# One stage of a hybrid decoder layer: a costed order of issue with GpSimd's instructions holding VectorE too, and normed tokens in natural order

## The chip, the cores and the metric

The kernel runs on one core of one Trainium2 chip. The metric is the device time of one execution in microseconds (us), as the median of several runs. A core has TensorE (PE, with its weight loads as PEld), VectorE (DVE), ScalarE (ACT), GpSimd (POOL), SyncE (SP) and 16 DMA engines. Each engine runs its own instructions in the order in which the program issued them; it waits at an instruction whose operands another engine has not finished.

## What is computed

A decoder layer on 2048 tokens of width 1024: two token mixers share an input projection (they end before the stage spoken of here), then an output projection with a residual, a norm, a router and a mixture of 64 small gated MLPs, two for each token:

```
rwkv7_mixer:  y = groupnorm(y) * ln_w + ln_b;  return (y + bonus) * g        # 512 wide, 8 heads
y_mix = concatenate([y_rw, y_fox]);  x = x + y_mix @ w_out
h = rms_norm(x, norm_ffn_w)
g_sel = argmax(h @ rg_w + rg_b)                 # one of 8 groups
top_p, top_i = top_k(softmax((h @ re_w + re_b)[g_sel]), 2)
x = x + sum over the 2 experts e of gate_e * (silu(h @ w_gate[e]) * (h @ w_up[e])) @ w_down[e]
```

## The kernel before

Products are made in float16 from pairs: a value is split into a high half (a cast) and a low half (value minus high), and three products of halves are summed. The kernel ends with two stages that matter here.

The first is `mix`, from about 1390 to 1705 us. It works through 16 tiles of 128 tokens. For each tile: GpSimd makes the bonus term (L1547, L1548); `head_norm` normalises the heads on DVE (L1493 to L1508); GpSimd applies the norm's weight and adds the bonus (L1568, L1569); DVE multiplies by the gate (L1573); ACT and DVE split the result into halves (L1576, L1578), PE transposes it (L1584) and multiplies it by the output weights (L1625 to L1627); DVE adds the residual (L1639); ACT squares and sums (L1650), small DVE steps make the inverse root, and L1661 writes the normed tile `h32` (128 tokens by 1024, float32). ACT casts `h32` into the high half (L1669) and DVE subtracts to get the low half (L1671). Both read `h32` through a rearranged view, so that the halves lie k-major: element n = 8q + k goes to place (k, q). The halves are stored to memory (`h2d`, L1683), and PE transposes them in 8 blocks of 128 contiguous columns each, 16 transposes a tile (L1686); the tile is the stationary operand (a weight load), the identity the moving one. The router's products (L1695, L1697) give logits, `place` picks groups and experts on DVE (L1712 to L1765), and GpSimd scatters each token's entry into a table (L1769).

The order of issue in `mix` is not that of the code. `Lanes` holds generators; each yields what it needs next: an engine with a cost in us (`"D", 0.6` is 0.6 us of VectorE, P GpSimd, A ScalarE, T TensorE), a buffer, or a mark of other work. The recorder keeps a clock for each engine and always issues the step that can start first by these costs; steps that tie go by the order of the lanes. The costs are written by hand and decide nothing but the order; on the chip, each engine takes the order as it stands.

The second is `experts`, from about 1730 us to the end, with a recorder of its own. For each of 64 experts: an indirect DMA gathers up to 112 tokens' halves from `h2d` into `XG`; PE transposes them, 8 blocks for each half, 16 an expert (L2110); DVE copies them out (L2113); ACT and DVE split the weights, of which each expert has 12 pieces of 128 by 1024 (L1975 high, L1979 low); PE multiplies (L2152 to L2154, then L2145 to L2147). The weights stream from memory all the while. Four of the L1979 steps of the first experts are issued inside `mix`, at its end (`split_first`), and the lines L1973 and L1975 likewise.

Of the kernel before, what the change touches and what calls it, by code (L numbers as in the profile page):

```python
# [12 lines left out]
AF = mybir.ActivationFunctionType  # L13
# [6 lines left out]
D = 1024  # L20
# [9 lines left out]
SL = 112  # L30
# [13 lines left out]
class Lanes:  # L44

    def __init__(self, slots, order=()):
        self.lanes = {k: [] for k in order}  # L50
        self.free, self.marks, self.end = {}, {}, 0.0
        self.slots = {k: [0.0] * n for k, n in slots.items()}
# [22 lines left out]
    def run(self):  # L75
        while any(self.lanes.values()):
            best = None
            for q in self.lanes.values():
                if q:
                    what, t = q[0][1], q[0][2]  # L80
                    if isinstance(what, tuple):
                        t = max(t, self.free.get(what[0], 0.0))
                    elif what in self.slots:
                        if not self.slots[what]:
                            continue
                        t = max(t, self.slots[what][0])
                    elif what in self.marks:
                        t = max(t, self.marks[what])
                    else:
                        continue  # L90
                    if best is None or t < best[0]:
                        best = t, q, what
            t, q, what = best
            if isinstance(what, tuple):
                self.free[what[0]] = t + what[1]
                t += what[1] + (0.13 if what[0] != "T" else 0)
            elif what in self.slots:
                self.slots[what].pop(0)
            q[0][2] = self.end = t
            self.step(q)  # L100


class Kern:
# [1410 lines left out]
    def mix(self):  # L1514
# [13 lines left out]
        with ExitStack() as es:  # L1528
# [10 lines left out]
            def bonus(i):  # L1539
# [4 lines left out]
                yield f"vt{i}"  # L1544
                yield "P", 2.2
                s["bo"] = bo = wf.tile([128, 512], F32, name="gbo")
                nc.gpsimd.tensor_tensor(h8(bo), h8(V), bc(bon), op=OP.mult)  # L1547
                nc.gpsimd.tensor_tensor(bo, bo, row["rw_ln_b"], op=OP.add)  # L1548
                lanes.mark(f"bo{i}")
# [7 lines left out]
            def gate(i):  # L1557
# [8 lines left out]
                yield f"bo{i}"  # L1566
                yield "P", 2.5
                nc.gpsimd.tensor_tensor(y, y, row["rw_ln_w"], op=OP.mult)  # L1568
                nc.gpsimd.tensor_tensor(y, y, s["bo"], op=OP.add)  # L1569
                lanes.mark(f"y{i}")  # L1570
                yield "D", 0.6
# [3 lines left out]
                yield "A", 0.52  # L1575
                nc.scalar.activation(yh[:, 0], y, AF.Copy)  # L1576
                yield "D", 0.6
                TT(yh[:, 1], y, yh[:, 0], op=OP.subtract)  # L1578
# [52 lines left out]
            def residual(i, hf):  # L1631
                s = St[i]
                if hf == 0:
                    if i >= 2:
                        yield f"normed{i - 2}"
                    s["xm"] = xms[:, i % 2]
                yield "D", 0.6
                c = slice(hf * 512, hf * 512 + 512)
# [6 lines left out]
            def route(i):  # L1645
# [10 lines left out]
                yield "D", 0.08  # L1656
                for _ in self.rsqrt1_steps(wk, r, s["ss"]):
                    yield "D", 0.08
# [6 lines left out]
                yield "A", 0.95  # L1665

                h16 = h16s[:, i % 2]
                hv = h32.rearrange("p (q k) -> p k q", k=KB)
                nc.scalar.activation(h16[:, 0], hv, AF.Copy)  # L1669
                yield "D", 1.2  # L1670
                nc.vector.tensor_tensor(h16[:, 1], hv, h16[:, 0], op=OP.subtract)  # L1671
                lanes.mark(f"low{i}")
                lanes.start("logits", logits(i, h16))

            def logits(i, h16):
# [3 lines left out]
                for m in range(2):  # L1679
                    yield "sm"  # L1680
                    yield "T", 0.45
                    if m == 0:
                        nc.sync.dma_start(self.h2d[i * 128:(i + 1) * 128], h16.rearrange("p s k q -> p (s k q)"))  # L1683
# [3 lines left out]
                    yield "A", 0.9  # L1687
                    nc.scalar.activation(hT[:, m], pt, AF.Copy)
# [19 lines left out]
            def place(i, lg):  # L1708

                yield "D", 0.08  # L1710
                m8 = wk.tile([128, 8], F32, name="m8")
                nc.vector.max(m8, lg[:, 0:8])  # L1712
                yield "D", 0.08
                i8 = wk.tile([128, 8], U32, name="i8")
                nc.vector.max_index(i8, m8, lg[:, 0:8])
                yield "D", 0.08
# [4 lines left out]
                yield "D", 0.13  # L1721
                pen = wk.tile([128, 8], F32, name="pen")
                TS(pen, iof[:, 0:8], gf, -1e30, op0=OP.not_equal, op1=OP.mult)
                yield "D", 0.13
# [3 lines left out]
                yield "D", 0.13  # L1728
# [3 lines left out]
                yield "D", 0.13  # L1732
                e8 = wk.tile([128, 8], U32, name="e8")
# [26 lines left out]
                lanes.give("sm")  # L1760
                yield "D", 0.08
                STT(pos, pos, float(E), ef, op0=OP.mult, op1=OP.add)
                yield "D", 0.08
                ri = wk.tile([128, 2], I32, name="ri", bufs=2)
# [9 lines left out]
            def weigh(i, lg, ng, zz):  # L1774
# [4 lines left out]
                nc.scalar.activation(zz, zz, AF.Exp)  # L1779
                yield "D", 0.08  # L1780
                dn = wk.tile([128, 1], F32, name="dn")
                TS(dn, zz[:, 1:2], 1.0, sg, op0=OP.add, op1=OP.mult)
                yield "D", 0.08
                nc.vector.reciprocal(dn, dn)
                yield "D", 0.08
                TS(ent[:, i, :, 1], zz, dn, None, op0=OP.mult)
# [252 lines left out]
    def experts(self, pools, jobs, out):  # L2039
# [61 lines left out]
        def transpose(e):  # L2101
# [3 lines left out]
            for s in range(2):  # L2105
# [183 lines left out]
```

## Time and profile before

| | |
|---|---|
| median of 3 runs | 2910.86 us (2909.12 to 2910.91) |
| profiled execution | 2912.27 us, span 2910.5 us |
| PE busy over the span | 2578.2 us (89%) |
| DVE busy over the span | 2389.0 us (82%) |
| ACT, POOL busy over the span | 1755.2 us (60%), 809.3 us (28%) |
| `mix`, steady part | 14 tiles in 252.7 us |
| DMA | 222 GB/s over the span |

The span is the time between the first and the last instruction of the profiled execution; its device time lies 1.8 us above it. Busy shares are means over stages that differ, so a stage is read by its own window, and what ended the idle time before an instruction says whom it waited for.

### The profile page before, as it was taken

The page shows a single profiled execution, that of the slowest core. Times are in us where ns is not written, and L with a number is a line of the kernel's source. Part 1 is how long each engine was busy: PE and PEld are TensorE (multiplying, and loading weights), DVE is VectorE, ACT ScalarE, POOL GpSimd, SP SyncE. Part 2 cuts the span into 40 slices and gives each one's busy share as a digit, 9 for nine tenths or more (in the row PEclk, how much of TensorE's full clock was granted, in tenths as well). Part 3 has the DMA queues.
Part 4 walks back from the last instruction along what each step waited for, and adds up shares of the span by engine and source line. Part 5 has one row for each costly group of instructions (what it writes and reads, how often), then busy time and mean ns, then how long its engine had stood idle before and what let it go on. Part 6 is the DMA issues. An engine that isn't in the chain of part 4 may idle for free. (4 is left out here: it accounts for less than half of the span.)

```text
span 2910.5 us, 52852 instructions
## 1 busy us (share of the span) xinstructions
PE 2578.2 (89%) x20309; PEld 1456.2 (50%) x20309; DVE 2389.0 (82%) x4277; ACT 1755.2 (60%) x2470; POOL 809.3 (28%) x728
## 2 busy tenths in 40 slices
PE   4987878799999999999887849999999999999997
PEld 2554544444445545544344425555565555555554
DVE  6779898873567788787989868888888999999997
ACT  5443434422234555556344438888878888888886
POOL 2211211133024545456545432111111111111110
PEclk7999999899999999999999969999999999999999
DMA  5343433533336444342464459999999999999996
GB/s 177 126 157 116 141 126 131 184 95 114 100 86 156 123 89 120 89 110 65 162 227 168 141 192 351 358 371 334 364 341 359 351 374 371 372 374 376 373 382 224
DMA packets 276599, 645.43 MB, mean 222 GB/s; under 512 B 134380, under 2 KB 192090, under 8 KB 251000
## 3 DMA queue, kind: packets, MB, share of 16 engines
q1 hardware_dynamic: 257256, 603.69, 58.6%
q0 software_dynamic: 18640, 38.22, 5.5%
q8 instruction: 160, 2.62, 0.4%
q14 instruction: 95, 0.78, 0.1%
q10 hardware_dynamic: 448, 0.12, 0.0%
HBM read 541.34 MB, written 111.16 MB: 224 GB/s over the span
## 5 line engine op out<-in xcount | busy, mean ns | idle before, releaser
L2208 POOL DMA_INDIRECT out_dram<-o,idx x64 | 123.5, 1930 | 775.3 <-ACT o L2202 771.6
L1979 DVE SCALAR_TENSOR_TENSOR wh<-st,wh 128x1024 f16<-128x1024 f32 x224 | 270.7, 1230 | 14.3 <-ACT wh L1975 14.3
L1241 POOL TENSOR_TENSOR acc<-acc,P 128x128 f32<-128x128 f32 (+6 forms) x288 | 236.5, 841 | 163.2 <-ACT P L1204 152.7
L1979 DVE SCALAR_TENSOR_TENSOR h<-st,h 128x1024 f16<-128x1024 f32 x240 | 278.7, 1233 | 0.8 <-ACT h L1975 0.8
L1204 ACT ACTIVATE P<-st,biasT 128x512 f32<-128x512 f32 (+3 forms) x320 | 184.8, 621 | 152.6 <-PE st L1194 70.1
L1975 ACT ACTIVATE h<-st 128x1024 f16<-128x1024 f32 x240 | 243.4, 1047 | 28.0 <-PE pd L2147 27.9
L1975 ACT ACTIVATE wh<-st 128x1024 f16<-128x1024 f32 x222 | 221.8, 1052 | 45.4 <-PE gu L2154 44.4
L2153 PE MATMUL gu<-wh,XT 128*112 128x512 f16 x512 | 194.0, 379 | 38.8 <-DVE wh L1979 38.4
L2145 PE MATMUL pd<-h,HT 128*112 128x512 f16 x504 | 191.9, 381 | 30.5 <-ACT HT L2187 30.5
L2154 PEld LDWEIGHTS <-XT 128*112 128x112 f16 x1024 | 132.6, 130 | 145.9 <-issue 66.6
L1162 DVE TENSOR_REDUCE mx<-na 128x1 f32<-128x512 f32 (+3 forms) x296 | 171.2, 604 | 33.3 <-PE na L1074 22.9
L2152 PE MATMUL gu<-wh,XT 128*112 128x512 f16 x512 | 194.9, 381 | 0.0
L279 PE MATMUL mm<-rwh,hT 128*128 128x512 f16 (+1 forms) x512 | 185.6, 363 | 10.0 <-DVE pk L654 7.5
L2154 PE MATMUL gu<-wh,XT 128*112 128x512 f16 x512 | 194.2, 379 | 0.0
L2146 PE MATMUL pd<-h,HT 128*112 128x512 f16 x504 | 191.0, 379 | 0.5 <-DVE h L1979 0.4
L2147 PE MATMUL pd<-h,HT 128*112 128x512 f16 x504 | 191.0, 379 | 0.0
L280 PE MATMUL mm<-rwl,hT 128*128 128x512 f16 (+1 forms) x512 | 185.3, 362 | 4.3 <-DVE rwl L259 4.3
L281 PE MATMUL mm<-rwh,hT 128*128 128x512 f16 (+1 forms) x512 | 184.7, 361 | 0.9 <-ACT hT L635 0.9
L2153 PEld LDWEIGHTS <-XT 128*112 128x112 f16 x1024 | 133.4, 130 | 73.6 <-issue 0.2
L2152 PEld LDWEIGHTS <-XT 128*112 128x112 f16 x1024 | 133.0, 130 | 73.5
L1226 PE MATMUL O<-P,Vp 128*64 128x512 f32 (+3 forms) x640 | 158.9, 554 | 2.3 <-ACT P L1204 2.2
L279 PE MATMUL mm<-fwh,hT 128*128 128x512 f16 (+1 forms) x512 | 157.5, 330 | 1.6 <-ACT vt L370 1.6
(445 smaller groups left out, 6823.2 us busy)
## 6 DMA issues: line engine op xcount, KB each, us to landing
st<-in_exp_w_up_dram SPq DMA_DIRECT2D x55, 2048.0 KB
st<-in_exp_w_down_dram SPq DMA_DIRECT2D x54, 2048.0 KB
st<-in_exp_w_gate_dram SPq DMA_DIRECT2D x51, 2048.0 KB
pkd<-pk SPq DMA_DIRECT2D x16, 1740.0 KB
xt<-in_x_dram SPq DMA_DIRECT2D x32, 512.0 KB
wst<-in_exp_w_gate_dram SPq DMA_DIRECT2D x32, 512.0 KB
d<-mp SPq DMA_DIRECT2D x48, 224.0 KB
hTd<-hT SPq DMA_DIRECT2D x16, 512.0 KB
```

The source lines that it names most:

```text
L279: nc.tensor.matmul(ps, xh(k), wh(k), start=(k == 0), stop=False)
L280: nc.tensor.matmul(ps, xh(k), wl(k), start=False, stop=False)
L1204: nc.scalar.activation(P[:, :n], ps[:, :n], AF.Exp, bias=self.bias[:, g, kb, 2 * hp + s:2 * hp + s + 1])
L1241: e.tensor_tensor(acc, acc, P[:, lo:hi], op=OP.add)
L1975: self.nc.scalar.activation(h[:, 0], st, AF.Copy, scale=WS)
L1979: self.nc.vector.scalar_tensor_tensor(h[:, 1], st, WS, h[:, 0], op0=OP.mult, op1=OP.subtract)
L2145: nc.tensor.matmul(pd[s], HT[:, 0, q], h[:, 0, c], start=(q == 0), stop=False)
L2146: nc.tensor.matmul(pd[s], HT[:, 0, q], h[:, 1, c], start=False, stop=False)
L2147: nc.tensor.matmul(pd[s], HT[:, 1, q], h[:, 0, c], start=False, stop=(q == 3))
L2152: nc.tensor.matmul(p, XT[:, 0, x], h[:, 0, k], start=(x == 0), stop=False)
L2153: nc.tensor.matmul(p, XT[:, 0, x], h[:, 1, k], start=False, stop=False)
L2154: nc.tensor.matmul(p, XT[:, 1, x], h[:, 0, k], start=False, stop=(x == KB - 1))
```

## The change

Three things. First, in the recorder a step may name several engines: GpSimd's four instructions a tile are now single steps `"PD", 1.3`, which start when both GpSimd and VectorE are free by the recorder's clock and take up both. Second, the costs of the other steps in `mix` are rewritten. Third, `h16` is stored in natural order: ACT and DVE read `h32` and write the halves as they lie, and the transposes of PE, here and in the expert loop, pick every eighth column of the tile.

```diff
@@ Lanes.run
-                        t = max(t, self.free.get(what[0], 0.0))
+                        t = max([t] + [self.free.get(e, 0.0) for e in what[0]])
...
-                self.free[what[0]] = t + what[1]
+                for e in what[0]:
+                    self.free[e] = t + what[1]
@@ bonus (gate the same, from "P", 2.5)
-                yield "P", 2.2
+                yield "PD", 1.3
                 s["bo"] = bo = wf.tile([128, 512], F32, name="gbo")
                 nc.gpsimd.tensor_tensor(h8(bo), h8(V), bc(bon), op=OP.mult)
+                yield "PD", 1.3
                 nc.gpsimd.tensor_tensor(bo, bo, row["rw_ln_b"], op=OP.add)
@@ route
-                yield "D", 0.08
+                yield "D", 0.12
...
-                yield "D", 1.2
+                yield "D", 1.25
                 h32 = hh[:, 0]
                 STT(h32, s["xm"], r, nfw, op0=OP.mult, op1=OP.mult)
...
-                yield "A", 0.95
-
-                h16 = h16s[:, i % 2]
-                hv = h32.rearrange("p (q k) -> p k q", k=KB)
-                nc.scalar.activation(h16[:, 0], hv, AF.Copy)
-                yield "D", 1.2
-                nc.vector.tensor_tensor(h16[:, 1], hv, h16[:, 0], op=OP.subtract)
+                yield "A", 1.02
+                h16 = h16s[:, i % 2].rearrange("p s k q -> p s (k q)")
+                nc.scalar.activation(h16[:, 0], h32, AF.Copy)
+                yield "D", 1.25
+                nc.vector.tensor_tensor(h16[:, 1], h32, h16[:, 0], op=OP.subtract)
@@ logits
-                        nc.tensor.transpose(pt[:, k], h16[:, m, k], self.id16)
+                        nc.tensor.transpose(pt[:, k], h16[:, m].rearrange("p (q k) -> p k q", k=KB)[:, k], self.id16)
@@ experts.transpose
-                    nc.tensor.transpose(pt[:, k], XG[e % 3][:, s * D + k * 128:s * D + k * 128 + 128],
-                                        self.id16[:SL, :SL])
+                    x = XG[e % 3][:, s * D:s * D + D].rearrange("p (q k) -> p k q", k=KB)[:, k]
+                    nc.tensor.transpose(pt[:, k], x, self.id16[:SL, :SL])
```

The order moves on every engine in `mix`; in the expert loop no instruction changes its place. Lines of the changed kernel stand 2 to 4 higher (L1510 is the old L1508, L1577 the old L1573, L1665 L1661, L1673 L1671, L1705 L1702, L1982 L1979). Three places on VectorE follow. The first is one tile in the middle of the stage, from the last step of the head norm (`vt<-vt,grs`) to the gate's product (`vt<-vt,g`), which reads what GpSimd makes of it. Before:

```order
L1508 TENSOR_TENSOR vt<-vt,grs 128x512
L1702 SCALAR_TENSOR_TENSOR lgs<-lg,rb 128x72
L1661 SCALAR_TENSOR_TENSOR h_17172<-xm,rs,nfw 128x1024
L1712 MAX m_19359<-lgs 128x8
L1493 TENSOR_REDUCE gm<-vt 128x8
L1715 MAX_INDEX i_19367<-m_19359,lgs 128x8
L1495 SCALAR_TENSOR_TENSOR vt<-gm,vt 128x512
L1718 CAST gf<-i_19367 128x1
L1720 TENSOR_SCALAR ng<-m_19359 128x1
L1671 TENSOR_TENSOR h_17173<-h_17172,h_17173 128x1024
L1723 TENSOR_SCALAR pen<-iof,gf 128x8
L1573 TENSOR_TENSOR vt<-vt,g 128x512
```

and of the change:

```order
L1510 TENSOR_TENSOR vt<-vt,grs 128x512
L1658 TENSOR_SCALAR ss<-ss 128x1
L1495 TENSOR_REDUCE gm<-vt 128x8
L142 TENSOR_SCALAR rsq_i<-ss 128x1
L143 TENSOR_SCALAR rsq_g<-rsq_i 128x1
L1497 SCALAR_TENSOR_TENSOR vt<-gm,vt 128x512
L149 TENSOR_SCALAR rsq_a<-rsq_g,ss 128x1
L1705 SCALAR_TENSOR_TENSOR lgs<-lg,rb 128x72
L151 TENSOR_SCALAR rs<-rsq_a,rsq_g 128x1
L1715 MAX m_19538<-lgs 128x8
L149 TENSOR_SCALAR rsq_a<-rs,ss 128x1
L1577 TENSOR_TENSOR vt<-vt,g 128x512
```

The norm of the tile (L1661) and the low half (L1671) have left the stretch; small steps of the inverse root (`rsq`) stand in it. The second place is a tile's norm and what stands between it and the low half, which waits for ScalarE's cast; before:

```order
L1578 TENSOR_TENSOR yh<-vt,yh 128x512
L1765 CAST ri<-posv 128x2
L1661 SCALAR_TENSOR_TENSOR h_17172<-xm,rs,nfw 128x1024
L1495 SCALAR_TENSOR_TENSOR vt<-gm,vt 128x512
L1671 TENSOR_TENSOR h_17173<-h_17172,h_17173 128x1024
L1639 SCALAR_TENSOR_TENSOR xm<-mm,xt 128x512
L1500 TENSOR_REDUCE gv<-gsq 128x8
```

and of the change:

```order
L1665 SCALAR_TENSOR_TENSOR h_17172<-xm,rs,nfw 128x1024
L1734 MAX v_19577<-el 128x8
L158 TENSOR_SCALAR rsq_i<-gv 128x8
L159 TENSOR_SCALAR grs<-rsq_i 128x8
L1737 MAX_INDEX e_19592<-v_19577,el 128x8
L1739 TENSOR_TENSOR zz<-v_19577 128x2
L1673 TENSOR_TENSOR h_17173<-h_17172,h_17173 128x1024
```

Where one step of the next tile's head norm stood, five short steps of another tile's placing stand now. The third is the end of the stage; before, from the last tile's low half on (`lgs<-lg,rb` is the last tile's logits, and `el`, `v`, `e`, `zz`, `ef` are of the tile ahead of it):

```order
L1671 TENSOR_TENSOR h_17173<-h_17172,h_17173 128x1024
L1726 TENSOR_TENSOR el<-lgs,pen 128x64
L1979 SCALAR_TENSOR_TENSOR xt<-st_17178,xt 128x1024
L1731 MAX v_20560<-el 128x8
L1979 SCALAR_TENSOR_TENSOR xm<-st_17178,xm 128x1024
L1734 MAX_INDEX e_20589<-v_20560,el 128x8
L1736 TENSOR_TENSOR zz<-v_20560 128x2
L1979 SCALAR_TENSOR_TENSOR xt<-st_17178,xt 128x1024
L1740 CAST ef<-e_20589 128x2
L1702 SCALAR_TENSOR_TENSOR lgs<-lg,rb 128x72
```

and of the change, from the last tile's norm on:

```order
L1665 SCALAR_TENSOR_TENSOR h_17172<-xm,rs,nfw 128x1024
L1673 TENSOR_TENSOR h_17173<-h_17172,h_17173 128x1024
L1982 SCALAR_TENSOR_TENSOR xt<-st_17178,xt 128x1024
L1982 SCALAR_TENSOR_TENSOR xm<-st_17178,xm 128x1024
L1982 SCALAR_TENSOR_TENSOR xt<-st_17178,xt 128x1024
L1982 SCALAR_TENSOR_TENSOR xm<-st_17178,xm 128x1024
L1705 SCALAR_TENSOR_TENSOR lgs<-lg,rb 128x72
L1715 MAX m_20638<-lgs 128x8
```

The four low halves of expert weights (L1979) stood among the steps of placing tile 14; now that tile is placed before the last norm, and the four stand together behind the last low half.

## Rows read from the trace of the kernel before

**Rows 1.** The page's first part: each engine's busy time, its share of the span and its instructions.

```profile
PE 2578.2 (89%) x20309; PEld 1456.2 (50%) x20309; DVE 2389.0 (82%) x4277; ACT 1755.2 (60%) x2470; POOL 809.3 (28%) x728
```

**Rows 2.** The windows view: busy time of each engine (with its count of instructions) in two stretches: the steady part of the stage, from the first L1671 to the fifteenth (14 tiles), and 100 us of the expert loop. Columns: the stretch, its length, PE, PEld, DVE, ACT, POOL, granted clock, DMA share, GB/s.

```profile
1428.80:1681.50 252.70, 200.13 (x1391) 102.15 (x1391) 226.38 (x787) 110.11 (x156) 114.91 (x83) 0.97 0.53 185
...
2060.00:2160.00 100.00, 94.17 (x533) 58.38 (x532) 89.66 (x88) 82.56 (x93) 17.00 (x10) 1.00 0.99 366
```

**Rows 3.** The waits of DVE in the steady part of the stage (1428 to 1682 us): engine, line, waited for: us in total, times, longest.

```profile
DVE h L1671 <- ACT h L1669: 13.6, 10, 3.0
```

**Rows 4.** The timeline at the end of the stage and the start of the expert loop.

```profile
1689.89 2.00 DVE L1671 TENSOR_TENSOR h<-h,h 128x1024 f16<-128x1024 f32 x1 [1.02 <-ACT h L1669]
...
1692.74 1.21 DVE L1979 SCALAR_TENSOR_TENSOR xt<-st,xt 128x1024 f16<-128x1024 f32 x1
...
1697.20 1.20 DVE L1979 SCALAR_TENSOR_TENSOR xm<-st,xm 128x1024 f16<-128x1024 f32 x1
...
1700.96 0.23 DVE L1731 MAX8 v<-el 128x8 f32<-128x64 f32 x1
...
1703.63 0.17 DVE L1765 CAST ri<-posv 128x2 int32<-128x2 f32 x1
...
1705.37 0.96 POOL L1769 DMA_INDIRECT tab<-ent,ri  x1 [0.30 <-issue]
...
1718.12 3.85 POOL L2094 DMA_INDIRECT xg<-h2d,idx  x1 [11.62 <-issue]
...
1728.74 2.42 PE L2110 MATMUL pt<-id,xg 112*128 112x112 f16 x24 [25.06 <-DMA xg<-h2d,idx]
```

**Rows 5.** The groups of instructions by line in the stage (1390 to 1690 us), shapes kept apart. Columns: line, engine, operation, out<-in, shapes, count | busy us, mean ns of one | idle time of the engine before them and its releaser.

```profile
L1669 ACT ACTIVATE h<-h 128x1024 f16<-128x1024 f32 x16 | 32.9, 2059 | 25.6 <-DVE h L1661 25.6
...
L1671 DVE TENSOR_TENSOR h<-h,h 128x1024 f16<-128x1024 f32 x16 | 32.6, 2034 | 14.6 <-ACT h L1669 14.6
...
L1661 DVE SCALAR_TENSOR_TENSOR h<-xm,rs,nfw 128x1024 f32<-128x1024 f32 x16 | 24.6, 1540 | 0.1
...
L1979 DVE SCALAR_TENSOR_TENSOR wh<-st,wh 128x1024 f16<-128x1024 f32 x4 | 6.1, 1513 | 0.0
...
L1547 POOL TENSOR_TENSOR gbo<-vt 128x512 f32<-128x512 f32 x16 | 21.2, 1327 | 2.4 <-DMA vt<-pkd 1.3
...
L1569 POOL TENSOR_TENSOR vt<-vt,gbo 128x512 f32<-128x512 f32 x15 | 20.8, 1385 | 1.2
```

**Rows 6.** The same view of the expert loop (2060 to 2820 us): the split of a weight piece into its halves on ACT and DVE (natural order, 1024 elements), the activations' split (512 elements, read with a step of four), and two weight loads of TensorE, of 128 and of 112 columns.

```profile
L1979 DVE SCALAR_TENSOR_TENSOR h<-st,h 128x1024 f16<-128x1024 f32 x160 | 185.9, 1235 | 0.8 <-ACT h L1975 0.8
...
L1975 ACT ACTIVATE h<-st 128x1024 f16<-128x1024 f32 x160 | 160.0, 1044 | 4.7 <-PE pd L2147 4.7
...
L2176 ACT ACTIVATE h<-sl 112x512 f16<-112x512 f32 x43 | 48.6, 1131 | 38.0 <-DVE sl L2171 38.0
...
L2178 DVE TENSOR_TENSOR h<-sl,h 112x512 f16<-112x512 f32 x42 | 46.6, 1109 | 0.0
...
L2152 PEld LDWEIGHTS <-XT 128*112 128x112 f16 x670 | 86.8, 130 | 47.3
...
L2110 PEld LDWEIGHTS <-xg 112*128 112x128 f16 x672 | 41.4, 98 | 17.1
```

**Rows 7.** The timeline of two tiles, DVE, ACT and POOL, and one row of PE (eight transposes merged): start us, duration us, engine, line, operation, in brackets the idle time before it and its releaser.

```profile
1610.89 1.29 DVE L1661 SCALAR_TENSOR_TENSOR h<-xm,rs,nfw 128x1024 f32<-128x1024 f32 x1
...
1612.49 2.04 ACT L1669 ACTIVATE h<-h 128x1024 f16<-128x1024 f32 x1
...
1614.56 2.02 DVE L1671 TENSOR_TENSOR h<-h,h 128x1024 f16<-128x1024 f32 x1 [1.78 <-ACT h L1669]
...
1615.26 0.61 PE L1686 MATMUL pt<-id,h 128*128 128x128 f16 x8
...
1620.71 0.69 DVE L1508 TENSOR_TENSOR vt<-vt,grs 128x512 f32<-128x512 f32 x1
...
1621.64 1.26 POOL L1568 TENSOR_TENSOR vt<-vt,rw_ln_w 128x512 f32<-128x512 f32 x1 [6.71 <-DVE ss L1654]
...
1622.98 1.27 POOL L1569 TENSOR_TENSOR vt<-vt,gbo 128x512 f32<-128x512 f32 x1
...
1624.84 1.93 DVE L1661 SCALAR_TENSOR_TENSOR h<-xm,rs,nfw 128x1024 f32<-128x1024 f32 x1
...
1625.77 2.14 POOL L1548 TENSOR_TENSOR gbo<-gbo,rw_ln_b 128x512 f32<-128x512 f32 x1
...
1628.59 0.67 DVE L1573 TENSOR_TENSOR vt<-vt,g 128x512 f32<-128x512 f32 x1
```

**Rows 8.** The view of one line, here of two lines of DVE in the stage: count: shortest/median/longest duration in ns, first and last start, shapes.

```profile
L1661 DVE SCALAR_TENSOR_TENSOR h<-xm,rs,nfw x16: 1271/1286/2164, 1425.2 to 1685.6; 128x1024 f32<-128x1024 f32 x16
...
L1723 DVE TENSOR_SCALAR pen<-iof,gf x16: 219/738/1250, 1438.2 to 1700.4; 128x8 f32<-128x8 f32 x16
```

**Rows 9.** The timeline of TensorE at one slab's transposes in the expert loop (eight instructions of a kind merged into a row).

```profile
2000.41 0.56 PE L2110 MATMUL pt<-id,xg 112*128 112x112 f16 x8
...
2000.80 0.38 PE L2152 MATMUL gu<-wh,XT 128*112 128x512 f16 x1
```

**Rows 10.** The waits of TensorE in the expert loop: the first row from 1766 to 2100 us, the second from 2220 to 2820 us.

```profile
PE pd L2145 <- ACT HT L2187: 27.7, 18, 1.6
...
PE gu L2153 <- DVE wh L1979: 34.0, 97, 0.5
```

More of the change, by code (lines that the diff above doesn't have):

```diff
@@ L1566, in gate @@
                 yield f"bo{i}"
-                yield "P", 2.5
+                yield "PD", 1.3
                 nc.gpsimd.tensor_tensor(y, y, row["rw_ln_w"], op=OP.mult)
+                yield "PD", 1.3
                 nc.gpsimd.tensor_tensor(y, y, s["bo"], op=OP.add)
                 lanes.mark(f"y{i}")
-                yield "D", 0.6
+                yield "D", 0.66
                 yh = wf.tile([128, 2, 512], F16, name="yh")
@@ L1574, in gate @@
                 lanes.give("sm")
-                yield "A", 0.52
+                yield "A", 0.6
                 nc.scalar.activation(yh[:, 0], y, AF.Copy)
-                yield "D", 0.6
+                yield "D", 0.66
                 TT(yh[:, 1], y, yh[:, 0], op=OP.subtract)
@@ L1636, in residual @@
                     s["xm"] = xms[:, i % 2]
-                yield "D", 0.6
+                yield "D", 0.66
                 c = slice(hf * 512, hf * 512 + 512)
@@ L1652, in route @@
                 nc.sync.dma_start(out[i * 128:(i + 1) * 128], s["xm"])
-                yield "D", 0.08
+                yield "D", 0.12
                 TS(s["ss"], s["ss"], 0.5 / D, 0.5e-6, op0=OP.mult, op1=OP.add)
                 r = wk.tile([128, 1], F32, name="rs")
-                yield "D", 0.08
+                yield "D", 0.12
                 for _ in self.rsqrt1_steps(wk, r, s["ss"]):
-                    yield "D", 0.08
-                yield "D", 1.2
+                    yield "D", 0.12
+                yield "D", 1.25
                 h32 = hh[:, 0]
@@ L1664, in route @@
                     yield f"logits{i - 2}"
[L1665 to L1671 removed]
+                yield "A", 1.02
+                h16 = h16s[:, i % 2].rearrange("p s k q -> p s (k q)")
+                nc.scalar.activation(h16[:, 0], h32, AF.Copy)
+                yield "D", 1.25
+                nc.vector.tensor_tensor(h16[:, 1], h32, h16[:, 0], op=OP.subtract)
                 lanes.mark(f"low{i}")
@@ L1682, in logits @@
                     if m == 0:
-                        nc.sync.dma_start(self.h2d[i * 128:(i + 1) * 128], h16.rearrange("p s k q -> p (s k q)"))
+                        nc.sync.dma_start(self.h2d[i * 128:(i + 1) * 128], h16.rearrange("p s n -> p (s n)"))
                     pt = smp.tile([128, KB, 128], F16, name="pt", tag="sm")
                     for k in range(KB):
-                        nc.tensor.transpose(pt[:, k], h16[:, m, k], self.id16)
-                    yield "A", 0.9
+                        nc.tensor.transpose(pt[:, k], h16[:, m].rearrange("p (q k) -> p k q", k=KB)[:, k], self.id16)
+                    yield "A", 1.0
                     nc.scalar.activation(hT[:, m], pt, AF.Copy)
@@ L1708, in place @@
             def place(i, lg):
-                yield "D", 0.08
+                yield "D", 0.12
                 m8 = wk.tile([128, 8], F32, name="m8")
                 nc.vector.max(m8, lg[:, 0:8])
-                yield "D", 0.08
+                yield "D", 0.12
                 i8 = wk.tile([128, 8], U32, name="i8")
                 nc.vector.max_index(i8, m8, lg[:, 0:8])
-                yield "D", 0.08
+                yield "D", 0.12
                 gf = wk.tile([128, 1], F32, name="gf")
@@ L1720, in place @@
                 TS(ng, m8[:, 0:1], -1.0, None, op0=OP.mult)
-                yield "D", 0.13
+                yield "D", 0.15
                 pen = wk.tile([128, 8], F32, name="pen")
                 TS(pen, iof[:, 0:8], gf, -1e30, op0=OP.not_equal, op1=OP.mult)
-                yield "D", 0.13
+                yield "D", 0.15
                 el = wk.tile([128, 8, 8], F32, name="el")
@@ L1727, in place @@
                    op=OP.add)
-                yield "D", 0.13
+                yield "D", 0.15
                 elf = el.rearrange("p g e -> p (g e)")
@@ L1731, in place @@
                 nc.vector.max(v8, elf)
-                yield "D", 0.13
+                yield "D", 0.15
                 e8 = wk.tile([128, 8], U32, name="e8")
@@ L1760, in place @@
                 lanes.give("sm")
-                yield "D", 0.08
+                yield "D", 0.12
                 STT(pos, pos, float(E), ef, op0=OP.mult, op1=OP.add)
-                yield "D", 0.08
+                yield "D", 0.12
                 ri = wk.tile([128, 2], I32, name="ri", bufs=2)
@@ L1779, in weigh @@
                 nc.scalar.activation(zz, zz, AF.Exp)
-                yield "D", 0.08
+                yield "D", 0.12
                 dn = wk.tile([128, 1], F32, name="dn")
                 TS(dn, zz[:, 1:2], 1.0, sg, op0=OP.add, op1=OP.mult)
-                yield "D", 0.08
+                yield "D", 0.12
                 nc.vector.reciprocal(dn, dn)
-                yield "D", 0.08
+                yield "D", 0.12
                 TS(ent[:, i, :, 1], zz, dn, None, op0=OP.mult)
```

## The prediction

> **What bounds the kernel now.** I read the page's busy shares first: PE 89%, DVE 82% [rows 1]. They are means, so the windows view comes next. In the steady part of the stage DVE is busy 226.38 of 252.70 us, 90%, and PE only 200.13, while in the expert loop PE is busy 94.17 of 100 with DMA at 0.99 [rows 2]. So the changed stage is paced by VectorE, 252.70/14 = 18.05 us a tile, of which (252.70 - 226.38)/14 = 1.88 us is idle; the expert loop is paced by PE and the weight stream. The waits of DVE say what the idle time is: 13.6 us of 26.3 is L1671 waiting for ScalarE's cast L1669 [rows 3]. What the stage saves passes on one to one: its end is a chain from the last tile's places through the table to the first gather, and PE stands idle 25.06 us for that before its first transpose at 1728.74 [rows 4].
>
> **What is removed: the strided reads.** L1671 takes 2034 ns on DVE, L1669 2059 on ACT, both reading `h32` with a step of eight [rows 5]. The nearest natural rows, of the same 1024 elements, are L1979 at 1235 and L1975 at 1044 ns [rows 6]. On DVE, which paces, that is 16 x (2034 - 1235) = **-12.8 us**. The bound at the other end is L1979 where it runs in this stage, 1513 ns [rows 5]: -8.3. I take the first, since that row is of 160 instructions and the second of four.
>
> **The wait for the cast.** Now: L1661 ends at 1610.89 + 1.29 = 1612.18, the cast runs 1612.49 to 1614.53, and L1671 starts at 1614.56 after 1.78 us idle; the hand-overs are 0.31 + 0.03 us [rows 7]. With a natural cast the chain is 1.04 + 0.34 = 1.4 us in place of 2.4. The order of the change leaves some five short steps between the norm and the low half, none over the 0.23 us of the longest row of that kind [rows 4], so about 1.0 us of work, and 0.4 us of waiting, 16 times: 6.4 in place of 14.6 [rows 5], **-8.2 us**. Bounds: -14.6 where other work fills all of it, and -4 where hardly anything stands between.
>
> **The order.** GpSimd's four instructions a tile each take about 1.3 us (1327 and 1385 on average) [rows 5]. While one runs, some DVE instructions are held: L1661 took 1.93 us beside L1548, which itself took 2.14, against 1.29 in another tile [rows 7]. Over the stage L1661 has a mean of 1540 ns and a shortest of 1271, and L1723, with eight elements, 750 and 219 [rows 5, 8]: 16 x 0.27 + 16 x 0.53 = 12.8 us of holding in these two lines alone. The recorder now counts on this and keeps DVE free in its own clock while GpSimd works. But on the chip nothing is reserved: the same four instructions a tile run beside a DVE that is nine tenths busy, and whichever DVE instruction comes next is held. So I take the sum of the holds as it was, **0 us**; bounds -10, if most of the 12.8 goes, and +21, which is a rival below.
>
> At the end of the stage, the four L1979 of 1.2 us stood among the steps of placing tile 14, from 1692.74 to 1697.20 + 1.20, ahead of the last tile's scatters, which follow `ri` at 1703.63 [rows 4]. Now tile 14 is placed ahead of the last norm, and the four run while PE and ACT transpose and multiply the last tile for the router. In the old order 1.02 us is lost in front of the last L1671, and some ten small steps of tile 14, at up to 0.23 us, stand behind it [rows 4]; now these are out of the last chain. I take **-3 us**, between 0 and -5. SP's stores of `h2d` move a place or two against the weight loads in its queue; they are first read by the gather at 1718.12 [rows 4], some 20 us later, so 0 us. ACT's costs and the rest of the table change no work.
>
> **What is added: strided weight loads.** A transpose loads the tile as weights; the identity moves past it. Before, 128 neighbouring columns are loaded; now every eighth, in 16 transposes a tile and 16 an expert. The trace has no strided weight load, so it is bounded. Eight transposes in the expert loop take 0.56 us with 213 ns for the last [rows 6, 9], so they follow each other at (0.56 - 0.21)/7 = 50 ns, and a load of 128 columns lasts 98 ns where one of 112 columns lasts 130 [rows 6]. That the larger is the shorter says that a full load takes several columns at a time: if four, 32 positions against 112, the 32 ns between them are 80 positions of 0.4 ns. What a step of eight costs an engine's read can be seen on ACT and DVE: from 512 to 1024 strided elements (step four and eight) the time grows by 2059 - 1131 = 928 and 2034 - 1109 = 925 ns, 1.81 ns an element on both [rows 5, 6]. If TensorE's port paid that at each position, a strided load would be 32 x 1.81 = 58 ns, if two columns came at a time 116, if one 232. Below lies 50, no change. I take 58, nearest to the row that shows full loads shorter than 112 columns: 8 ns x 1024 = **+8.2 us** in the expert loop, where PE is busy 94% and the transposes stand in its queue between products (the next product starts at 2000.80, 0.39 after the first transpose) [rows 2, 9]. In the stage, at (0.61 - 0.22)/7 = 56 ns now [rows 7], it is 2 x 256 = **+0.5 us**, on an engine with 52 us of slack there. The bounds are 0 and, at 116 and 232 ns, 68 and 187 us in the loop.
>
> [...]
>
> **Sum.** -12.8 - 8.2 + 0 - 3 + 8.2 + 0.5 = -15.3 us. From the profiled 2912.27 us (its span is 2910.5) that is 2897.0; the median of the runs lies 1.4 below that execution, so **2896 us**. With the ends of the small terms (-8.3 to -12.8, -4 to -14.6, -10 to 0, 0 to -5, 0 to +8.2; the far loads apart) all at one end would give -42 and -4 us, 2869 to 2908; since they are not all at one end at once, the forecast's own range is 2876 to 2906.
>
> **Rivals.** *Strided loads are dear.* [...] It costs 66 x 1024 = 68 us or 182 x 1024 = 187 us in the loop, in place of 8.2: about 2896 + 59 = 2955 or, with some 20 us that the stage cannot hide, 3095 us. For it: ACT's and DVE's doubling at the same step [rows 5, 6], and that PE has no slack in the loop [rows 2]; its waits there are 27.7 us over 334 and 34.0 us over 600 [rows 10], about 60 us that could hide the first part of it. Against it: the short full loads. It decides from the point where a transpose costs 23 ns more (24.0 us of gain over 1024 transposes).
>
> *VectorE waits for GpSimd at the gate's product.* Before, L1508 ends at 1621.40, GpSimd's two instructions run from 1621.64 to 1624.25, and L1573 comes at 1628.59, with the norm and others between [rows 7]. In the change some 2.7 us of DVE work is between them, which is about what the two instructions take. If DVE stops there for one instruction of GpSimd, 1.3 us, in each of 16 tiles, that is +21: 2917 us, slower. Against it: small steps of `rsq` that are held too would make the stretch longer by themselves.
>
> *The holds take the gain back.* DVE's time beside GpSimd is lost whatever it runs; what was hidden beside the cast's wait is now met by busy instructions. If each L1671 is held as L1979 is in this stage (1513 - 1235 = 278 ns, 16 times, 4.5 us) and each L1661 goes to 1.93 us (0.39, 16 times, 6.2 us) [rows 5, 7], 11 us of 15 go: 2907 us, no change.
>
> **How the numbers follow.** A measurement of this kernel tells about 0.2%, 5.8 us, from no change, so "same" is 2905 to 2917. Forecast 0.58, half-rate loads 0.12, one column at a time 0.08, the wait for GpSimd 0.12, the holds 0.10. Faster: 0.57 of the forecast and 0.03 of the holds, 0.60; same: 0.01 + 0.07 + 0.05 of the wait for GpSimd, 0.13; slower: 0.20 + 0.07, 0.27. The range reaches from 2876 past the first rival's first case, to 2964; it leaves out the dearest loads (0.08) and the edges.
>
> **What the profile would show.** Right: L1671's successor (L1673) near 1.24 us and L1669's near 1.04; DVE's wait for that cast under 7 us; a tile in about 16.7 us; the first transposes of the loop some 23 us earlier; eight transposes of the loop within 0.6 us. Wrong: a transpose group of 1 us or more, or longer periods in the loop; a wait of L1577 for GpSimd of over a microsecond a tile; L1661 and L1673 well above 1.5 us on average.

## The result, and the profile after

The changed kernel takes 2934.49 us (2933.64 to 2934.85), the kernel before 2910.89 beside it: 0.81% slower, ratio 1.0081 [1.0064, 1.0099]. The forecast was 2896, faster. The time lies within the stated range (2876 to 2964), but on the other side. The slower half of that range was there for dear weight loads, and those are not what happened.

The loss is in the stage. The expert loop's first transpose starts at 1744.43 us, 15.7 us later than in [rows 4] where 23.5 us earlier was forecast; from there to the end of the span the loop takes 1188.0 us, 6.2 more than before (2910.5 - 1728.74 = 1181.8). The windows view of the changed kernel over the same 14 tiles as in [rows 2] (columns as there):

```profile
1425.50:1689.00 263.50, 207.34 (x1352) 105.69 (x1350) 205.52 (x786) 95.85 (x154) 103.35 (x82) 0.88 0.49 170
```

A tile takes 263.5/14 = 18.82 us, not 16.7. DVE is busy 205.52 us, less than before by 1.49 us a tile, so its work did become shorter; but it is idle 58 us where it was 26. The granted clock, here a mean of stretches at 1.00 (1560 to 1574 us, say) and at 0.50 (1576 to 1580 us), fell from 0.97 to 0.88. The groups by line (1380 to 1700 us), to read beside [rows 5]; the last two are products of the same tiles for the first and the second half of the output's columns, PE's first work after it waited and what follows:

```profile
L1643 DVE SCALAR_TENSOR_TENSOR xm<-mm,xt 128x512 f32<-128x512 f32 x31 | 21.4, 690 | 43.6 <-PE mm L1631 43.4
...
L1665 DVE SCALAR_TENSOR_TENSOR h<-xm,rs,nfw 128x1024 f32<-128x1024 f32 x15 | 19.4, 1293 | 0.0
...
L1673 DVE TENSOR_TENSOR h<-h,h 128x1024 f16<-128x1024 f32 x15 | 19.0, 1265 | 2.9 <-ACT h L1671 2.5
...
L1671 ACT ACTIVATE h<-h 128x1024 f16<-128x1024 f32 x15 | 15.8, 1055 | 9.3 <-DVE h L1665 9.2
...
L1629 PE MATMUL mm<-wo,yT 128*128 128x512 f16 x64 | 31.3, 489 | 14.3 <-ACT yT L1591 14.3
...
L1629 PE MATMUL mm<-wol,yT 128*128 128x512 f16 x64 | 24.3, 379 | 0.0
```

The forecast low half (L1673) is there, 1265 ns, and the cast, 1055. What is new is 43 us of DVE waiting at the residual (L1643) for PE's products. The waits of DVE in the stage, first more rows of the view of [rows 3] from the kernel before, then those of the change (1428 to 1690 us), and behind them the waits of PE in the change:

```profile
DVE xm L1639 <- PE mm L1627: 3.9, 5, 1.6
...
DVE lgs L1702 <- PE lg L1695: 1.2, 2, 1.0
...
DVE jk L1758 <- PE pos L1753: 0.8, 1, 0.8
```

```profile
DVE xm L1643 <- PE mm L1631: 30.5, 19, 2.6
...
DVE lgs L1705 <- PE lg L1698: 8.9, 12, 1.8
...
DVE jk L1761 <- PE pos L1756: 8.7, 8, 2.3
...
DVE h L1673 <- ACT h L1671: 2.5, 4, 0.8
...
DVE vt L1577 <- POOL vt L1573: 1.4, 2, 1.2
```

```profile
PE yt L1588 <- DVE yh L1582: 14.1, 11, 2.3
...
PE yt L1588 <- ACT yh L1580: 13.7, 9, 2.5
...
PE mm L1629 <- ACT yT L1591: 12.4, 12, 1.1
```

The wait for the cast, 13.6 us before, is 2.5, and the wait for GpSimd at L1577 (a rival) is 1.4. In their place DVE waits 30.5 us for the projection, 3.9 before, and 17.6 for logits and positions, 2.0 before, while PE waits for DVE and ACT. Two engines that wait for each other in turn are a loop, and the timeline of one tile shows it closed (some rows of four engines in order of time):

```profile
1605.39 0.69 DVE L1577 TENSOR_TENSOR vt<-vt,g 128x512 f32<-128x512 f32 x1 [0.28 <-POOL vt L1573]
...
1607.15 1.22 DVE L1582 TENSOR_TENSOR yh<-vt,yh 128x512 f16<-128x512 f32 x1
...
1608.43 0.56 PE L1588 MATMUL yt<-id,yh 128*128 128x128 f16 x7 [0.73 <-DVE yh L1582]
...
1609.03 1.02 ACT L1591 ACTIVATE yT<-yt 128x1024 f16<-128x1024 f16 x1 [2.23 <-PE yt L1588]
...
1610.11 0.39 PE L1629 MATMUL mm<-wo,yT 128*128 128x512 f16 x1 [1.11 <-ACT yT L1591]
...
1617.09 0.69 DVE L1643 SCALAR_TENSOR_TENSOR xm<-mm,xt 128x512 f32<-128x512 f32 x1 [0.80 <-PE mm L1631]
...
1619.00 0.69 DVE L1510 TENSOR_TENSOR vt<-vt,grs 128x512 f32<-128x512 f32 x1
...
1619.45 1.07 POOL L1772 DMA_INDIRECT tab<-ent,ri  x1 [0.30 <-issue]
...
1620.55 1.27 POOL L1571 TENSOR_TENSOR vt<-vt,rw_ln_w 128x512 f32<-128x512 f32 x1
...
1621.90 1.61 POOL L1573 TENSOR_TENSOR vt<-vt,gbo 128x512 f32<-128x512 f32 x1
...
1623.63 0.68 DVE L1577 TENSOR_TENSOR vt<-vt,g 128x512 f32<-128x512 f32 x1
```

Read it downwards: the gate's product at 1605.39, the low half of `yh`, the transposes, the cast of `yT`, PE's products from 1610.11 on, and at 1617.09 the residual's second half, for which DVE waited 0.80 us. Behind that, in DVE's queue, stands the **next** tile's head norm (L1510, 1619.00), which needs nothing of this tile; behind it GpSimd's two steps (after a scatter), and at 1623.63 the next gate's product. That is once around in 1623.63 - 1605.39 = 18.24 us, and in this order, with these durations, a tile cannot take less. In the kernel before, the next gate's product starts 2 to 13 us ahead of the end of this tile's second residual step (tiles 1 to 13), so two tiles overlap; in the change it starts 0.1 to 11.5 us behind it.

### The profile page after: what moved, and what is told of

It is laid out like the page before. It is cut to its first block, busy times and chain, and to the rows that moved or that the text cites. A ratio compares the mean times of both kernels' runs of the same rounds, so it can differ in the third digit from the quotient of the medians.

```text
span 2932.4 us, 52821 instructions
## 1 busy us (share of the span) xinstructions
PE 2597.4 (89%) x20309; PEld 1477.8 (50%) x20309; DVE 2365.0 (81%) x4277; ACT 1739.1 (59%) x2470; POOL 788.1 (27%) x728
## 5 line engine op out<-in xcount | busy, mean ns | idle before, releaser
L1982 DVE SCALAR_TENSOR_TENSOR wh<-st,wh 128x1024 f16<-128x1024 f32 x224 | 268.7, 1219 | 14.4 <-ACT wh L1978 14.4
L1982 DVE SCALAR_TENSOR_TENSOR h<-st,h 128x1024 f16<-128x1024 f32 x240 | 278.2, 1223 | 1.1 <-ACT h L1978 1.0
```

The lines of the kernel that those rows point to most:

```text
L1982: self.nc.vector.scalar_tensor_tensor(h[:, 1], st, WS, h[:, 0], op0=OP.mult, op1=OP.subtract)
```

## The experiments

Each is timed beside the kernel before; the runs are from four chips, on which the kernel before took 2908.8 to 2910.8 us. This table is worked out from the windows view of each profile, from the first to the 15th low half (14 tiles); each profile is of one execution, which can lie some us off the median (6 in e9, 7 in e14); "costs" is what one tile takes of DVE and of TensorE by the recorder's own numbers (the sum of the `"D"` and `"PD"`, and of the `"T"` steps of the code).

| kernel | costs D / T | us a tile | DVE busy | DVE idle | clock | expert loop starts | median us | ratio, interval |
|---|---|---|---|---|---|---|---|---|
| before | | 18.05 | 16.17 | 1.88 | 0.97 | 1728.7 | 2910.9 | |
| change | 17.2 / 13.4 | 18.82 | 14.68 | 4.14 | 0.88 | 1744.4 | 2934.5 | 1.0081 [1.0064, 1.0099] |
| e1 natural order alone | | 16.55 | 15.44 | 1.11 | 0.99 | 1705.9 | 2896.2 | 0.9948 [0.9932, 0.9965] |
| e2 order alone | 17.2 / 13.4 | 19.58 | 15.50 | 4.09 | 0.87 | 1754.3 | 2938.8 | 1.0099 [1.0082, 1.0116] |
| e3 no hold | 12.0 / 13.4 | 16.16 | 15.04 | 1.13 | 0.96 | 1704.2 | 2892.9 | 0.9938 [0.9921, 0.9954] |
| e4 loop contiguous | 17.2 / 13.4 | 18.82 | 14.69 | 4.13 | 0.88 | 1744.6 | 2926.7 | 1.0054 [1.0037, 1.0071] |
| e5 transposes between | 17.2 / 13.4 | 18.32 | 14.91 | 3.41 | 0.88 | 1736.3 | 2928.1 | 1.0065 [1.0048, 1.0082] |
| e6 warm | 17.2 / 13.4 | 18.45 | 14.77 | 3.68 | 0.94 | 1740.8 | 2931.6 | 1.0079 [1.0062, 1.0096] |
| e7 hold 0.45 | 13.8 / 13.4 | 16.43 | 14.90 | 1.52 | 0.95 | 1701.7 | 2895.8 | 0.9957 [0.9941, 0.9974] |
| e8 hold at gate | 14.6 / 13.4 | 15.76 | 13.90 | 1.85 | 0.96 | 1696.8 | 2889.1 | 0.9934 [0.9917, 0.9951] |
| e9 head norm ahead | 17.2 / 13.4 | 17.43 | 13.46 | 3.97 | 0.97 | 1717.9 | 2914.0 | 1.0013 [1.0003, 1.0022] |
| e10 head norm behind | 12.0 / 13.4 | 22.35 | 17.44 | 4.91 | 0.84 | 1794.6 | 2987.5 | 1.0273 [1.0256, 1.0290] |
| e11 e8, not the last two | 14.6 / 13.4 | 15.72 | 14.03 | 1.70 | 0.96 | 1694.8 | 2886.1 | 0.9921 [0.9905, 0.9938] |
| e12 gate, 0.45 | 12.9 / 13.4 | 15.60 | 14.69 | 0.92 | 0.98 | 1699.9 | 2889.4 | 0.9933 [0.9916, 0.9949] |
| e13 hold at bonus | 14.6 / 13.4 | 17.54 | 14.94 | 2.60 | 0.92 | 1734.4 | 2922.0 | 1.0031 [1.0018, 1.0043] |
| e14 DVE costs up | 17.2 / 13.4 | 18.19 | 14.57 | 3.62 | 0.90 | 1740.5 | 2938.3 | 1.0099 [1.0083, 1.0116] |
| e15 TensorE costs up | 17.2 / 18.1 | 17.17 | 14.81 | 2.36 | 0.96 | 1708.1 | 2895.4 | 0.9946 [0.9930, 0.9963] |

### Which part: natural order, or the order of issue

e1 is the kernel before with the edits of natural order and nothing else.

> The kernel before with natural order alone (casts, low halves and strided transposes as in the change; recorder and costs as before). Theory A, that the new order of issue makes each tile's chain serial and natural order does what was forecast: L1671 -12.8 us, its wait for the cast about -8 us, the expert loop +6 us, so about 2896 us (2890 to 2902). Theory B, that natural order itself does the harm in the stage (through TensorE's strided loads, or through what is late behind them): 2925 us or more.

It took 2896.16 us. Its window, and the two lines of DVE that the forecast spoke of:

```profile
1429.50:1661.30 231.80, 195.76 (x1393) 100.82 (x1391) 216.25 (x787) 96.45 (x156) 116.08 (x83) 0.99 0.58 200
```

```profile
L1661 DVE SCALAR_TENSOR_TENSOR h<-xm,rs,nfw 128x1024 f32<-128x1024 f32 x16 | 23.7, 1479 | 0.1
...
L1670 DVE TENSOR_TENSOR h<-h,h 128x1024 f16<-128x1024 f32 x16 | 20.4, 1276 | 3.7 <-ACT h L1668 3.7
```

So the part of the sum on natural order holds: L1671 gives 16 x (2034 - 1276) = 12.1 us, the wait falls from 14.6 to 3.7.

e2 is the change with these edits undone.

> The change with the halves k-major as before (strided reads on ACT and DVE, contiguous weight loads), so that only the recorder and its costs are new. Theory A: the order costs about 38 us, less what DVE's waits for TensorE can hide of the longer low half: 2928 to 2948 us, with DVE waiting over 30 us for the output projection. Theory B: about 2905 us, no harm from the order.

2938.81 us: the order alone costs 29 us. That is 4 us slower than the change: the expert loop starts 9.9 us later and, with neighbouring columns again, is 7.1 us shorter (1180.9 against 1188.0). The longer low half is not hidden in DVE's waits: DVE is busy 15.50 us a tile against 14.68 in the change and idle about as long, and a tile takes 0.76 us more.

```profile
1422.80:1696.90 274.10, 210.91 (x1359) 105.52 (x1357) 216.88 (x786) 110.43 (x154) 104.38 (x82) 0.87 0.48 163
```

Only the waits are shared out otherwise: 17.2 us at the residual, not the over 30 expected, and 12.3 for the cast.

e3 keeps the change but takes the hold away:

```diff
-                yield "PD", 1.3
+                yield "P", 1.3
```

> The change with GpSimd's steps holding GpSimd alone in the recorder (P in place of PD, 1.3 us each), all other new costs and natural order kept. Theory A1, that it is the hold of DVE in the recorder's clock that puts each tile's transposes right ahead of its own products: 2900 us or less, and DVE's wait for the projection falls from 36 to under 10 us. Theory A2, that the rewritten costs do it: about 2934 us.

2892.94 us, and DVE's wait for the projection is 7.8 us. The rewritten costs are harmless; the hold of DVE in the recorder's clock costs 41.6 us against this kernel.

### The loads of weights

e4 reads the expert loop's transposes from 128 neighbouring columns again, and leaves out putting the columns in the experts' order.

> The change, but the expert loop's transposes load 128 neighbouring columns as before (so the experts get their inputs' columns in a wrong order; the routing is untouched). If the strided load is what the loop lost: the loop is 6 us shorter, 2928 us, and eight transposes take 0.56 us again in place of 0.65. If something else in the loop did it: 2934 us.

2926.72 us, 7.8 less, and nothing else moved: the stage is the same to 0.2 us. One line's view, in the change and then in e4 (count, shortest/median/longest ns):

```profile
L2114 PEld LDWEIGHTS <-xg x1024: 140/153/169, 1744.4 to 2878.3; 112*128 112x128 f16 x171
...
L2114 PE MATMUL pt<-id,xg x1024: 214/225/316, 1744.4 to 2878.3; 112*128 112x112 f16 x171
```

```profile
L2113 PEld LDWEIGHTS <-xg x1024: 95/98/151, 1744.6 to 2870.5; 112*128 112x128 f16 x171
...
L2113 PE MATMUL pt<-id,xg x1024: 210/213/301, 1744.6 to 2870.5; 112*128 112x112 f16 x171
```

A strided load lasts 153 instead of 98 ns; the loop is 1188.0 - 1180.3 = 7.7 us longer for 1024 of them, 7.5 ns each. The forecast had 8.

### Why the hold costs 41 us

My first theory put it on TensorE: in the change the transposes of a tile stand right ahead of their own products, so PE waits for ACT's cast each time. e5 makes the second half of the products wait, in the recorder, for the next tile's transposes:

```diff
                         lanes.start("xm", residual(i, hf))
+                        if hf == 0 and i + 1 < NT:
+                            yield f"yT{i + 1}"
```

> The change, PD and all costs kept, but the second half of a tile's last products waits, in the recorder, for the next tile's transposed activations, so that these transposes stand between the two halves instead of right ahead of their own products. Theory A (each tile's chain is serial because its transposes stand right ahead of its own products): the loss of the order goes, 2893 to 2903 us, and TensorE's wait for the cast of the transposes (12.4 us) goes to about 0. Theory C, that the hold in the recorder harms by what it does to DVE's or GpSimd's order, whatever TensorE's order: 2920 us or more.

2928.08 us. PE's wait for the cast is gone, and DVE waits nearly as before (its waits, 1428 to 1680 us):

```profile
DVE xm L1645 <- PE mm L1631: 24.6, 15, 3.4
...
DVE lgs L1707 <- PE lg L1700: 8.2, 9, 1.7
```

That the loss stays looks like the end of the theory, but e5 does not decide it, since its edit makes a hand-over of its own: the second half's products stand on PE behind the next tile's transposes, and these waited for DVE's low half (rows of the timeline).

```profile
1562.28 0.93 PE L1588 MATMUL yt<-id,yh 128*128 128x128 f16 x7 [2.59 <-DVE yh L1582]
...
1563.00 0.63 PE L1629 MATMUL mm<-wol,yT 128*128 128x512 f16 x1
...
1568.44 0.69 DVE L1645 SCALAR_TENSOR_TENSOR xm<-mm,xt 128x512 f32<-128x512 f32 x1 [3.40 <-PE mm L1631]
```

Two thirds of the 24.6 us at the residual are now ahead of its second half. e6 asked about the clock, with idle work ahead of the transposes:

```diff
+                for _ in range(24):
+                    nc.tensor.transpose(pt[:, 0, 0], self.id16, self.id16)
```

> The change with 24 transposes of the identity ahead of each tile's eight, into the same buffer (overwritten), where TensorE idles about 1.7 us a tile. Theory D, that the lower granted clock behind the pause is a cost of its own: the first products after it go back from 490 to about 385 ns and the time falls by up to 15 us, to 2920. Theory A, where the chain's waits are what counts and TensorE's clock is a part of it: the same direction, but no more than 5 to 10 us. No gain, or a loss: the extra transposes are themselves in the chain and outweigh the clock.

2931.60 us, 3 us less. The granted clock rose to 0.94 and the first products to

```profile
L1631 PE MATMUL mm<-wo,yT 128*128 128x512 f16 x63 | 26.8, 425 | 14.6 <-ACT yT L1593 14.6
```

425 ns, and most of the loss stayed. What the lower clock alone costs is not separated from the added work: from 1426 to 1686 us PE is busy 218.67 us, 206.45 in the change.

e9 and e10 try the loop through DVE's queue that the timeline shows, from both sides. e9 keeps the hold and puts the next head norm ahead of both residual steps; e10 takes e3, which has no hold, and puts it behind both:

```diff
@@ e9: residual, first half (norm marks headed{i} at its end)
+                if i + 1 < NT:
+                    yield f"headed{i + 1}"
@@ e10: norm, ahead of the head norm's last step
+                        yield f"xm{i - 1}"
```

> The change, PD and all costs kept; in the recorder a tile's first residual step waits for the next tile's head norm, so that this head norm stands on DVE ahead of both residual steps instead of behind them. Theory E (in the change DVE's queue closes a loop: the head norm of the next tile stands behind the residual of this one, GpSimd and the gate behind the head norm, the transposes and products behind the gate, and the next residual behind those, 18.2 us around): the loop loses the part from the head norm to GpSimd's end, a tile takes 16 to 16.5 us and the time is 2895 to 2905 us, although on TensorE the transposes still stand right ahead of their products. Theory A (TensorE's order is the cause) or any other: 2925 us or more.

> The kernel of the third experiment (GpSimd alone in the recorder, 2893 us), made to put each tile's head norm behind both residual steps of the tile before on DVE. Theory E: the loss comes back without any hold in the recorder, a tile takes 18 us or more, 2920 to 2935 us. If the hold harms in another way: stays at 2893 to 2900 us.

e9 took 2914.01 us, half of the loss back; e10 2987.54, 95 us more than e3 without any hold. The direction is as the loop has it, both sizes are not. The waits of DVE in e9, then in e10, say where the rest is:

```profile
DVE lgs L1708 <- PE lg L1701: 26.6, 13, 2.7
...
DVE xm L1646 <- PE mm L1632: 3.4, 1, 3.4
```

```profile
DVE lgs L1708 <- PE lg L1701: 36.1, 14, 5.2
...
DVE xm L1646 <- PE mm L1634: 21.8, 13, 5.4
```

In e9 the wait at the residual fell from 30.5 to 3.4 us, and one of 26.6 came at the logits (L1708), the next instruction in DVE's queue that needs PE. In e10 both waits add up. Nor does the head norm's place decide by itself. In the change the next tile's head norm ends behind at least one residual step in 12 of 13 tiles (tiles 1 to 13). In e5 it does so in none, so this loop is open, and a tile still takes 18.32 us; in e8, further down, it does so in 9, and a tile takes 15.76. The loop of the timeline is thus one form of the loss and not its cause. What these orders seem to share is a habit and not one wrong place: what depends on another engine is issued soon behind its source.

A reason for the habit may lie in the costs. With the holds the recorder books DVE for 17.2 us a tile and TensorE for 13.4, so by its clock TensorE and ACT have time to spare, and a hand-over to them costs nothing. On the chip DVE is busy 14.68 us a tile in the change and PE 207.34/14 = 14.81. Five runs tell the sum of DVE's bookings from the holds and their places.

```diff
@@ e7: Lanes.run
-                    self.free[e] = t + what[1]
+                    self.free[e] = t + (0.45 if e == "D" and what[0] != "D" else what[1])
@@ e8: both steps of bonus (e13: both of gate instead)
-                yield "PD", 1.3
+                yield "P", 1.3
@@ e14 (on e3, scale {"D": 1.43} in mix), e15 (on the change, scale {"T": 1.35}): Lanes.run
+                cost = what[1] * self.scale.get(what[0], 1.0)
```

> The change with GpSimd's instructions holding DVE in the recorder for 0.45 us instead of 1.3 (about what the trace shows of holding, 1.75 us a tile over four). If the cost of the order comes from a DVE that the recorder thinks fuller than it is (17.2 us a tile by the costs, against 13.4 of TensorE): most of the loss goes, 2895 to 2910 us. If any hold at all does the harm: 2930 us.

> The change with the hold kept for the two gate instructions and taken from the two bonus instructions. Tells which of the two the loss comes from: about 2930 us if the gate's, which lie in the tile's chain, 2895 us if the bonus's, in between (2905 to 2920) if it is the sum of the recorder's DVE time (14.6 us a tile by the costs).

> The change with the hold kept for the two bonus instructions and taken from the two gate instructions (the mirror of the eighth experiment). Theory F (the loss comes when the recorder's DVE time a tile, 17.2 us with all holds, stands clear above TensorE's 13.4): DVE's time is 14.6 as in the eighth experiment, so about 2890 to 2900 us. If the hold at the bonus is harmful by itself: 2925 us or more.

> The kernel of the third experiment (no hold, 2893 us) with every DVE cost of this stage's recorder times 1.43, which brings DVE's time a tile to the 17.2 us that it has with the holds, with GpSimd out of it. Theory F: the loss comes back, 2915 to 2935 us, with DVE waiting 20 us or more for TensorE. If the hold's places do it and not the sum: 2893 to 2900 us.

> The change, all four holds kept, with every TensorE cost of this stage's recorder times 1.35, 18.1 us a tile, above DVE's 17.2 again. Theory F: the loss goes, 2888 to 2903 us. If the holds do harm whatever TensorE's time: 2925 us or more.

e14 brings the loss back with no hold at all (2938.31 us), and e15 takes it away with all four holds kept (2895.43). The waits of DVE in e14 and then in e15:

```profile
DVE xm L1645 <- PE mm L1633: 21.6, 21, 3.9
```

```profile
DVE h L1675 <- ACT h L1673: 9.1, 10, 1.1
...
DVE xm L1645 <- PE mm L1633: 1.1, 3, 0.4
```

21.6 us at the residual against 1.1. So the bookings of the two engines are shown to make and to undo the loss: DVE well above TensorE does it without any hold, and with TensorE above DVE the four holds cost 2.5 us against e3. Of the 36 us by which e15's expert loop starts earlier than in the change, 23 are in the 14 tiles (17.17 us a tile) and 13 between the last two low halves (7.2 us for 20.0). e7 (13.8 booked, 2895.77 us) fits.

The sum is not the whole rule. e8 and e13 both book 14.6. By the sum e8 was expected at 2905 to 2920 us, and it took 2889.14, nearer to the 2895 expected if the loss came from the bonus's holds; e13, with those alone, took 2922.03, above the 2890 to 2900 expected by the sum and 29 us above e3. DVE's wait for the projection in the 14 tiles, in e8 and then in e13:

```profile
DVE xm L1643 <- PE mm L1631: 7.7, 10, 2.9
```

```profile
DVE xm L1643 <- PE mm L1631: 15.5, 10, 5.6
```

Where the hold stands counts too. Why the bonus's holds cost 33 us more than the gate's was not settled. Each of these runs is one order, and none varies the ratio in small steps, so where the loss sets in is not known either.

### A faster kernel

e11 is e8 with `("PD" if i < NT - 2 else "P"), 1.3`; e12 is e8 with 0.45 us of hold.

> The kernel of the eighth experiment (hold at the gate only, 2889 us), without the hold in the last two tiles, where the last low half came 20.8 us behind the one before, against 8.2 us in the third experiment. If the hold delays the end there: 2 to 10 us faster, 2879 to 2887 us. If the last tile is bound by its own chain: no change, 2889 us.

> The hold at the gate only, as long as the trace shows GpSimd holding DVE (0.45 us an instruction, in place of 1.3). If the gain of the eighth experiment over the third comes from shorter holds of DVE (13.9 us busy a tile against 15.0), which need the full 1.3 in the recorder: back to 2893 us. If from the recorder's DVE time alone: 2889 us or less.

e11 is the fastest, 2886.09 us, ratio 0.9921 [0.9905, 0.9938], though its step over e8 (3 us) is small against the spread of e8's runs (2885.57 to 2894.50). Its last low half still comes 17.5 us behind the one before it, against 8.2 in e3. In e8 and e9 DVE is busy 13.9 and 13.5 us a tile against 15.0 in e3, which would fit a GpSimd that runs more while DVE has nothing to do; that overlap was not measured. With 0.45 us (e12) DVE is busy 14.7, and yet e12 took 2889.42 us, as long as e8: the shorter busy time is not what e8 gained over e3, and the intervals of e3, e8 and e12 overlap. One instruction did take longer beside GpSimd: L1661 took 1.93 us beside L1548 and 1.29 elsewhere [rows 7]; its mean of 1540 ns [rows 5] is 1293 in the change.

## Why the prediction was wrong, step by step

- **The strided reads removed, -12.8 us:** right; 12.1 in e1.
- **The wait for the cast, -8.2:** right in kind; -10.9 in e1, -12.1 in the change (14.6 to 2.5).
- **Strided loads, +8.2 in the loop:** right; 7.7 (e4). For the 58 ns I assumed four columns at a time; no run shows how many a load takes. The runs show 153 ns a load against 98. The case of a loop longer by 68 or 187 us did not come.
- **The order, 0 with bounds -10 to +21:** this is the step that failed. Against e1 the order made the expert loop start 38.5 us later: 14 x (18.82 - 16.55) = 31.8 us in the steady part, 13.3 more between the last two low halves (20.0 us against 6.7), 4.0 less ahead of the first and 2.5 less behind the last. In the steady part DVE's waits for PE (projection, logits, positions) grew from 5.9 to 48.1 us. I took "nothing is reserved on the chip" for "nothing changes", counted only holds and the wait of the gate's product for GpSimd, gave PE 52 us of slack without asking when DVE needs its results, and did not follow the moved rows across engines. The rows of the first place shown ahead of the prediction had a part of it: the tile's norm and low half had left the stretch between the head norm and the gate. That the head norm stands behind the residual is not in those rows, but it was in the order. The bound of +21 was the price of one GpSimd instruction a tile; waits for PE had no term in the sum at all (e10: 95 us). Why the booked costs give such an order is shown in part only (e14 and e15 for it, e8 and e13 beside it).
- **The end of the stage, -3:** right behind the last low half (38.9 to 35.5 us), but the last low half itself came later.
- **The rivals:** the wait of DVE for GpSimd was 1.4 us, not 21. The holds did not take the gain back; DVE's busy time fell from 16.17 to 14.68 us a tile, of which the natural low half is 0.77. None of the rivals was DVE waiting for PE.
- With the order at 0 the sum is 2896 us, and e1, which has no new order, took 2896.16. In part that is luck: the -3 us for the end belonged to the order, and without them the sum is 2899; the larger gain at the cast made up for it.

## What to carry to other kernels

The costs by which an order is made are also an idea of which engine paces. Here DVE booked well above TensorE gave an order in which DVE waited 21.6 us for the products (e14), and TensorE booked above DVE one in which it waited 1.1 (e15), though both sums of e15 lie above the measured busy time: the relation counted, and the place of a hold besides it (e8, e13). So when costs change, add them up by engine and compare the sums with each other and with the measured busy time. In the new order look, for each instruction that waits for another engine, at what independent work stands behind it in its queue and could stand ahead of it, and follow the moved rows on every engine before taking an order's price as nothing.

## What the runs showed of the hardware

A load of 128 float16 columns with a step of eight lasted 153 ns against 98 for neighbouring ones, but the expert loop grew only by 7.5 ns for each of them (e4). On ACT, a read of float32 with a step of eight took 2059 ns and 1055 without it; on DVE 2034 and 1265. The 153 ns lie below the 232 that the prediction estimated for one column at a time, but the strided form is not free.
